# A two-layer encoder: first weights in three pieces, an earlier key remainder, and half of the up weights in other buffers

## The chip, the cores and the metric

The kernel runs on one core of one Trainium2 chip. The metric is the device time of one execution in microseconds (us); the time before is the median of three runs.

## The reference

Two layers, each a mixer (latent attention beside a convolution branch) and a gated feed-forward, on 1024 tokens of width 1024, all in float32; then a last RMS norm.

```python
p = rmsnorm(x, g_mix) @ w_in                       # queries' latent, keys' latent, key rope, conv input
c_q, c_kv = rmsnorm(p[..., :384]), rmsnorm(p[..., 384:640])
q, kv = c_q @ w_uq, c_kv @ w_ukv                   # 8 heads; k_nope and v come out of kv
y_attn = softmax(q k^T * scale) v
u = silu(layernorm(dwconv31(a * sigmoid(gt))))     # a, gt: the last columns of p
x = x + concat(y_attn, u) @ w_o
zg, zv = split(dwconv3(rmsnorm(x, g_ffn) @ w_up))  # 2 x 2816 columns
x = x + (silu(zg) * zv) @ w_down
```

## The kernel before

**Arithmetic.** A float32 product is made of three matrix products: weights and moving data are split into a high part (suffix h) and a remainder, or low part (suffix l), and hh, hl and lh are added up in PSUM. ACT casts the high part, DVE subtracts to get the low part (some weights go through ACT and an accumulating DMA of POOL instead). On TensorE (PE) nearly all matmuls are 128x128 by 128x512.

**Order of the work.** The order on PE, DVE, ACT and POOL is that in which the program is written (a planner keeps a clock for DVE in `project`, and a table of steps is filled by `put(step, rank, ...)` in the feed-forward). Only the order of SP, which issues the plain loads and stores, is set by a scheduler. An engine works strictly in its order, so an instruction that waits holds all that stand behind it.

**Buffers.** Large tiles lie in four pools of equal slots: "b" with 31 slots of 512 KB, "m" with 8, "wr" with 3, "ws" with 8 (`SLOTS`). A new tile takes the slot that its pool's plan gives it and waits until the last reader of the tile before it is through.

**Start** (`first_sections`, L398 to L510). Three weight blocks g0, a0 and g1 are loaded raw, cast and lowered in two column pieces, 0:256 (`some`) and 256:1024 (`rest`). x comes in eight blocks; `upper_x` (ACT, L432) and `lower_x` (DVE, L435) split block k into xs_kh and xs_kl. PE runs the products of block 0 for all three weights (L489), then block by block (L534).

**Keys** (`key` in `project`, L687 to L699). pk_j, the j-th of four products, is cast to kh_j by ACT (L692) and lowered to kl_j by DVE (L694). A step tells the planner of DVE how long it takes and after how long the next may follow; the `yield 0.0, 1.0` between cast and lowering lets it put one tap of the convolution (L1727, 1.28 us) between. pu, the next product, takes the PSUM buffer of pk_1. qss (L242) is the queries' sum of squares, which PE turns (rq0t, L261).

**Up stage** (`up_steps`, L1017 to L1224). The product with w_up is made for 22 column blocks f, each with seven half-size products i in the order 1, 5, 6, 3, 7, 2, 4 (12 matmuls each, so 84 per f), from sums and differences of quarters of the weights. `fetch(f, e)` (L1041) loads the two raw halves wu_f0 and wu_f1 into "wr" slots; `combine(f, ...)` (DVE, L1037) makes the differences in place, and the first of them, `combine(f, 0, 0, 2)`, needs both halves. `part` and `cast` make the split weights w_f_i. `evict` copies or adds a product's PSUM bank into zg_f and zv_f (ACT at L1096 to L1111, DVE at L1037); product 3 adds into the bank of product 5 and so cannot begin before `evict(5, f)` (ACT, L1099) has copied it. `filter_start`, `filter_tap`, `silu` and `close` make v_f, which SP stores (act<-v, L1136). Beside it DVE makes sums sd_j of the down weights, which SP loads (L1141) and stores again (ws<-sd, L1149).

A name such as wu0_140 in the orders below is layer 0, f = 14, half 0.

Of the kernel before, what the change touches and what calls it, by code (L numbers as in the profile page):

```python
# [16 lines left out]
T = 1024  # L17
# [65 lines left out]
HALVES = (slice(0, 512), slice(512, T))  # L83
# [38 lines left out]
class Encoder:  # L122
# [274 lines left out]
    def first_sections(self, l, supply):  # L397
        nc, par = self.nc, self.par[l]  # L398
        names = ("g0", "a0", "g1")
        w = [(self.tmp("wr", f"w{n}{l}r"), *(self.tmp("b" if n == "g0" else "ws", f"w{n}{l}{i}", F32R) for i in "hl"))  # L400
             for n in names]
        x, acc = [self.blk(f"x{k}") for k in range(8)], self.blk(f"xss{l}")
        hl = [[self.tmp("m", f"xs{l}_{k}{i}", F32R) if k >= 4 else self.blk(f"xs{l}_{k}{i}", F32R) for i in "hl"]
              for k in range(8)]
        ps = [self.wide(f"p{n}{l}") for n in names]
        every, left, right = slice(0, T), *HALVES
        some, rest = slice(0, 256), slice(256, T)
        nc.sync.dma_start(out=w[0][0][:, some], in_=self.weight_source(l, names[0])[:, some])
        warm = self.bank("warm")[:, 0:128]
        for _ in range(WARM):  # L410
            nc.tensor.matmul(warm, self.ones, self.ones, start=True, stop=True)
        nc.scalar.activation(out=self.cp.tile([128, 1], F32, name="table"), in_=self.ones[:, 0:1], func=AF.Square)

        def load(i, c):
            nc.sync.dma_start(out=w[i][0][:, c], in_=self.weight_source(l, names[i])[:, c])

        def load_x(k, c=every):
            nc.sync.dma_start(out=x[k][:, c], in_=self.xd[0][k][:, c])

        def cast(i, c, on_vector=False):  # L420
            raw, hi, _ = w[i]
            (nc.vector.tensor_copy if on_vector else nc.scalar.copy)(out=hi[:, c], in_=raw[:, c])

        def lower(i, c):
            raw, hi, lo = w[i]
            nc.vector.tensor_tensor(out=lo[:, c], in0=raw[:, c], in1=hi[:, c].bitcast(F32), op=ALU.subtract)

        def part(k, c):
            return self.first[:, 8:520] if k == 0 and c == left else x[k][:, c]

        def upper_x(k, c=every):
            nc.scalar.activation(out=hl[k][0][:, c], in_=part(k, c), func=AF.Copy, scale=self.first[:, k:k + 1])  # L432

        def lower_x(k, c=every):
            nc.vector.scalar_tensor_tensor(out=hl[k][1][:, c], in0=part(k, c), scalar=self.first[:, k:k + 1],  # L435
                                           in1=hl[k][0][:, c].bitcast(F32), op0=ALU.mult, op1=ALU.subtract)

        def square(k):
            for c in (left, right) if k == 0 else (every,):
                self.sumsq(acc[:, c], part(k, c), k, f"xsq{l}_{k}")  # L440

        load_x(0, right)
        load(1, some)
        load(2, some)
        load_x(1)
        load(2, rest)
        load(0, rest)
        load(1, rest)
        for k in range(2, 8):
            load_x(k)  # L450
        self.ident = self.const("ident", [128, 128], self.a["ident"])
        nc.vector.tensor_copy(out=self.ones_r, in_=self.ones)
        nc.sync.dma_start(out=self.par[0], in_=self.a["par"][0])
        self.par += [self.const(f"par{i}", [128, NPAR], self.a["par"][i]) for i in range(1, DEPTH)]
        self.gfin = self.const("gfin", [128, 8], self.a["g_final"])
        upper_x(0, left)
        cast(0, some, True)
        upper_x(0, right)
        cast(1, some)
        lower_x(0, left)  # L460
        lower_x(0, right)
        lower(0, some)
        lower(1, some)
        cast(2, some)
        lower(2, some)
        upper_x(1)
        lower_x(1)
        cast(2, rest)
        lower(2, rest)
        cast(0, rest)  # L470
        lower(0, rest)
        cast(1, rest)
        upper_x(2)
        lower(1, rest)
        lower_x(2)
        square(0)
        upper_x(3)
        lower_x(3)
        square(1)
        for k in range(4, 8):  # L480
            upper_x(k)
            lower_x(k)
            square(k - 2)
        square(6)
        square(7)
        w = [e[1:] for e in w]
        for i, p, q in ((0, 0, 0), (0, 0, 1), (1, 0, 0), (1, 0, 1), (0, 1, 0), (1, 1, 0), (2, 0, 0), (2, 0, 1), (2, 1, 0)):
            for c in HALVES:
                nc.tensor.matmul(ps[i][:, c], w[i][p][:, 0:128], hl[0][q][:, c], start=p + q == 0, stop=False)  # L489
        nc.gpsimd.tensor_copy(out=self.cp.tile([128, 1], F32, name="held"), in_=x[2][:, 0:1])  # L490
        order = [(1, i) for i in range(3)] + [(k, i) for k in range(2, 8) for i in range(3)]
        supply(-8.0, 8.0)
        for k, i in order:
            self.partial(ps[i], self.tiled(w[i]), hl, k, upper=i == 0 and k < 4)
            if (k, i) == (5, 2):
                dg = self.rsqrt_cols(acc, D, f"rx{l}", HALVES, self.bank, turned=True)
            if (k, i) == (6, 2):
                rx = self.blk(f"rx{l}")
                for s, r in zip(HALVES, self.spread(dg, f"rx{l}", HALVES, self.bank)):
                    nc.scalar.copy(out=rx[:, s], in_=r)  # L500
        supply(-8.0)
        return hl, rx, dict(zip(names, ps))
# [34 lines left out]
    def project(self, l, carry):  # L537
        nc, a = self.nc, self.a
# [3 lines left out]
        gates, ckv, kvs, cq, cqs, vs, w = {}, [], [], [], [], [], {}  # L542
# [144 lines left out]
        def key(j):  # L687
            if j == 0:
                heads.update((h, self.head_tiles(l, h)) for h in range(DIRECT))
            p = ps[f"k{j}"]  # L690
            kh, kl = self.blk(f"kh{l}_{j}", F32R), self.blk(f"kl{l}_{j}", F32R)
            nc.scalar.copy(out=kh, in_=p)  # L692
            yield 0.0, 1.0
            nc.vector.tensor_tensor(out=kl, in0=p, in1=kh.bitcast(F32), op=ALU.subtract)  # L694
            for i, s in enumerate((kh, kl)):
                self.move(kd[i][2 * j:2 * j + 2].rearrange("h d t -> (h d) t"), s)
                for h in range(DIRECT if j == 0 else 0):
                    self.move(heads[h][1][i][0:NOPE, :], s[h * NOPE:(h + 1) * NOPE, :])
                    self.move(heads[h][1][i][NOPE:96, :], krd[i])  # L699
            yield 1.22, 0.0  # L700
# [119 lines left out]
        hl, rx, ps = self.first_sections(l, supply) if l == 0 else self.next_sections(l, carry, supply)  # L820
# [208 lines left out]
    def up_steps(self, l, steps, put):  # L1029
        nc, a = self.nc, self.a  # L1030
        left, right = HALVES
# [7 lines left out]
        def fetch(f, e, tag="wr"):  # L1039
            raw[f][e] = self.tmp(tag, f"wu{l}_{f}{e}")  # L1040
            nc.sync.dma_start(out=raw[f][e], in_=a["w_up"][l, f + e * NF])  # L1041
# [4 lines left out]
        def combine(f, o, p, q, op=ALU.subtract):  # L1046
            z = quarters(f)
            sub(z[o], z[p], z[q], op)
# [12 lines left out]
        def cast(i, f):  # L1061
            e, h = {1: (0, 0), 2: (0, 1), 4: (1, 1)}[i]
            casts[i, f] = self.cast_pair(a["w_up"][l, f + e * NF][:, HALVES[h]], f"w{l}_{f}_{i}", "b" if i == 4 and f >= LEFT else "ws")
# [90 lines left out]
        for f in range(1, LEFT):  # L1154
            n = 10 + f if f == 1 else 11 + f
# [4 lines left out]
        for q, (i, f) in enumerate(seq):  # L1160
            n = base + q
# [13 lines left out]
        for f in range(LEFT, NF):  # L1175
            n = at[1, f]
            for e in range(2):
                put(n - 8, 5, lambda f=f, e=e: fetch(f, 1 - e))
            put(n - 5, 3, lambda f=f: combine(f, 0, 0, 2))
            put(n - 4, 3, lambda f=f: combine(f, 2, 2, 3, ALU.add))  # L1180
            put(n - 3, 2, lambda f=f: part(5, f))
            put(n - 3, 2.1, lambda f=f: combine(f, 2, 3, 0))
            put(n - 2, 2, lambda f=f: part(6, f))
            put(n - 2, 2.1, lambda f=f: combine(f, 1, 1, 2))
            put(n - 2, 2.2, lambda f=f: part(3, f))
            put(n - 1, 2, lambda f=f: part(7, f))
        for f in range(NF):
            n = max(at[2, f], at[3, f], at[6, f]) + 1
# [11 lines left out]
        for j in range(NF // 2):  # L1200
            n = at[1, 7 + j * 13 // 11]
# [688 lines left out]
```

## Time and profile before

| | us |
|---|---|
| median of 3 runs (range) | 2277.66 (2277.26 to 2278.66) |
| the profiled execution | 2278.46 |
| its span | 2276.7 |
| PE busy in the span | 2268.5 (100%) |
| DVE / ACT / POOL busy | 1722.5 / 1287.4 / 782.5 |

Of the profiled time, 1.76 us lie around the span. In a row of the timeline the first number is the start in us, the second the duration, then engine, line of the kernel and operation, out<-in, size and count; what stands in brackets is the idle time of that engine just before, and what ended it. PEld is the load of weights into PE, which runs ahead of the matmuls; an idle time on it that ends in another engine's work is a stall of PE. SPq is SP's issue of a DMA. A line's number can be that of a helper: L1037 is every DVE addition or subtraction of the up stage.

### The profile page before, as it was taken

Reading aid. Unit: us, or ns where it says so; the run is one execution under the profiler, and the core shown is the slowest. Engines: PE = TensorE matmul, PEld = TensorE weight load, DVE = VectorE, ACT = ScalarE, POOL = GpSimd, SP = SyncE. Lnnn points to the kernel's source line nnn. Section 1 sums busy time; section 2 is a strip of 40 time slices with the busy share of each in tenths; the row PEclk is TensorE's granted clock in tenths of the full one; section 3 lists DMA queues with packets and bytes.
Section 4 is the critical chain, followed back from the end, with each engine's and each line's share of the span. In section 5 each row is a group of like instructions: output and inputs, shape, how many; then the busy total and the mean of one; then the engine's idle time right before and its main releaser. Section 6 shows DMA issues by size and latency. Waiting matters only on the chain.

```text
span 2276.7 us, 30491 instructions
## 1 busy us (share of the span) xinstructions
PE 2268.5 (100%) x10682; PEld 1887.5 (83%) x10682; DVE 1722.5 (76%) x2296; ACT 1287.4 (57%) x2047; POOL 782.5 (34%) x812
## 2 busy tenths in 40 slices
PE   9999999999999999999999999999999999999998
PEld 8888888888888888888888888888888888888887
DVE  6988888768877776776559788886697777768765
ACT  5355877646655555544533468774475555555444
POOL 1222797532333333001412237873323333320032
PEclk9999999999999999999999999999999999999999
DMA  6889998856899998935968999967659999988356
GB/s 192 167 180 266 201 205 171 213 154 138 208 283 293 277 294 207 335 105 140 210 137 167 218 254 199 186 149 211 173 131 233 269 299 273 299 214 316 102 122 170
DMA packets 198713, 475.73 MB, mean 209 GB/s; under 512 B 27184, under 2 KB 34848, under 8 KB 198560
## 3 DMA queue, kind: packets, MB, share of 16 engines
q0 software_dynamic: 103136, 222.46, 48.7%
q1 hardware_dynamic: 95136, 250.80, 33.1%
q8 instruction: 84, 1.38, 0.2%
q14 instruction: 69, 0.57, 0.1%
q10 hardware_dynamic: 288, 0.53, 0.1%
HBM read 309.29 MB, written 80.40 MB: 171 GB/s over the span
## 4 chain that ended last, share of the span: by engine, by line
PE 91%; DVE 4%; DMA 2%; issue 2%; ACT 1%; POOL 0%; DVEq 0%; POOLq 0%; ACTq 0%; SPq 0%
PE p L1088 33%; PE pd L1276 18%; PE s L1529 8%; PE po L899 6%; PE o L1581 5%; PE t L1558 5%; PE pa L222 2%; PE pg L222 2%; DVE conv L1727 2%; PE pg L534 2%; PE pq L222 1%; PE pn L222 1%; PE pv L1507 1%; PE pkv L222 1%; PE pa L534 1%
## 5 line engine op out<-in xcount | busy, mean ns | idle before, releaser
L1088 PE MATMUL p<-b,w 128*128 128x512 f32 x3552 | 806.8, 389 | 0.3 <-DVE zv L1037 0.2
L1088 PEld LDWEIGHTS p<-b,w 128*128 128x128 f32 x3552 | 666.3, 188 | 140.2 <-DVE w L1467 0.8
L1276 PE MATMUL pd<-ab,wd 128*128 128x512 f32 (+1 forms) x1920 | 422.3, 381 | 0.0
L1276 PEld LDWEIGHTS pd<-ab,wd 128*128 128x128 f32 x1920 | 350.7, 188 | 69.5 <-DVE ab L1467 0.4
L186 POOL DMA_DIRECT2D w<-wu x96 | 84.9, 887 | 360.9 <-ACT w L185 319.2
L1529 PE MATMUL s<-k,q 96*128 96x512 f32 x768 | 207.6, 405 | 0.0
L1561 DVE TENSOR_TENSOR pt<-t,pt 128x512 fp32r<-128x512 f32 x256 | 165.0, 686 | 53.2 <-ACT pt L1560 51.8
L1744 POOL TENSOR_TENSOR late<-gate,par 128x1014 f32<-128x1014 f32 (+12 forms) x79 | 171.3, 2168 | 19.0 <-DVE qn L734 9.8
L1560 ACT CAST pt<-t 128x512 fp32r<-128x512 f32 x256 | 137.8, 589 | 66.2 <-PE t L1558 62.6
L1479 DVE SCALAR_TENSOR_TENSOR o<-zg,par,o 128x1023 f32<-128x1023 f32 x88 | 112.7, 1283 | 79.3 <-ACT o L1473 77.9
L186 POOL DMA_DIRECT2D w<-in_w_up x116 | 100.5, 866 | 198.7 <-ACT w L185 181.6
L1531 DVE TENSOR_REDUCE mx<-s 128x1 f32<-128x1024 f32 x128 | 155.7, 1216 | 0.6 <-PE s L1529 0.6
L1529 PEld LDWEIGHTS s<-k,q 96*128 96x128 f32 x768 | 135.4, 189 | 23.1
L1539 ACT ACTIVATE p<-s,mx 128x1024 f32<-128x1024 f32 x128 | 144.9, 1132 | 1.2 <-DVE mx L1531 1.2
L1727 DVE SCALAR_TENSOR_TENSOR conv<-gate,par,conv 128x1009 f32<-128x1009 f32 (+7 forms) x112 | 142.3, 1274 | 3.6 <-ACT conv L596 1.0
L1581 PE MATMUL o<-pt,v 128*128 128x512 f32 x512 | 140.8, 398 | 0.0
L862 POOL DMA_DIRECT2D wd<-in_w_down x44 | 33.0, 755 | 307.5 <-PE pd L1276 301.7
L1465 ACT CAST ab<-ac 128x512 fp32r<-128x512 f32 x130 | 80.0, 617 | 98.2 <-DVE ac L1211 95.5
L185 ACT ACTIVATE w<-w 128x512 fp32r<-128x512 f32 x212 | 133.6, 630 | 3.0
L1558 PEld LDWEIGHTS t<-ident,p 128*128 128x128 f32 x1024 | 119.9, 141 | 18.2 <-ACT p L1539 0.4
L1558 PE MATMUL t<-ident,p 128*128 128x128 f32 x1024 | 133.0, 273 | 0.0
L1037 DVE TENSOR_TENSOR zg<-p,zg 128x512 f32<-128x512 f32 x88 | 60.5, 689 | 89.4 <-PE p L1088 82.4
(2105 smaller groups left out, 4105.1 us busy)
## 6 DMA issues: line engine op xcount, KB each, us to landing
w<-in_w_up POOLq DMA_DIRECT2D x232, 256.0 KB, 7.3
wu<-in_w_up SPq DMA_DIRECT2D x88, 512.0 KB, 6.0
w<-wu POOLq DMA_DIRECT2D x96, 256.0 KB, 5.5
sd<-in_w_down SPq DMA_DIRECT2D x44, 512.0 KB, 10.3
ws<-sd SPq DMA_DIRECT2D x44, 512.0 KB, 7.9
wd<-in_w_down POOLq DMA_DIRECT2D x88, 256.0 KB, 5.4
act<-v SPq DMA_DIRECT2D x36, 512.0 KB, 5.8
ac<-act SPq DMA_DIRECT2D x72, 256.0 KB, 6.1
```

The source lines that it names most:

```text
L186: self.nc.gpsimd.dma_start(out=lo, in_=src, accum_op=ALU.add)
L222: nc.tensor.matmul(ps[:, HALVES[c]], w, x[:, HALVES[c]], start=(k == 0 and s == 0), stop=(k == n - 1 and s == 2))
L1088: nc.tensor.matmul(ps, w[p][:, k * 128:(k + 1) * 128], b[:, q], start=(i in (1, 5, 2) and k == 0 and t == 0), stop=(k == 3 and t == 2), sk ...
L1276: nc.tensor.matmul(ps[t, m][:, cs], w[i, j][p][:, m * 128:(m + 1) * 128], b[:, q, cs], start=(i in (1, 5, 2) and j == 0 and s == 0), stop= ...
L1529: nc.tensor.matmul(ps[:, cs], q[i][0:96, qs], k[j][0:96, cs], start=(s == 0), stop=(s == 2))
L1531: nc.vector.tensor_reduce(out=mx, in_=ps, op=ALU.max, axis=AX.X, negate=True)
L1539: nc.scalar.activation(out=p, in_=ps, func=AF.Exp, bias=mx, accum_out=st["sums"][:, qt:qt + 1])
L1558: nc.tensor.transpose(tp[:, i, qi * 128:(qi + 1) * 128], st["p"][2 * qp + qi][:, kt * 128:(kt + 1) * 128], self.ident)
L1561: nc.vector.tensor_tensor(out=lo, in0=tp, in1=hi.bitcast(F32), op=ALU.subtract)
L1581: nc.tensor.matmul(po, v[2 * c + i][:, h // 2, e, :], pt[s][:, i, :], start=(c == 0 and i == 0 and s == 0), stop=(c == 3 and i == 1 and s ...
L1727: self.nc.vector.scalar_tensor_tensor(out=y[:, lo:hi], in0=u[:, lo + s:hi + s], scalar=self.tap(l, j, t), in1=y[:, lo:hi], op0=ALU.mult, o ...
L1744: self.nc.gpsimd.tensor_tensor(out=p[:, lo:hi], in0=u[:, lo + s:hi + s], in1=self.tap(l, j, t).broadcast_to([128, hi - lo]), op=ALU.mult)
```

## The change

Four edits:

1. The raw weights of the start come in three column pieces (0:256, 256:512, 512:1024), so nine loads, casts and lowerings instead of six, and in another order between the loads of x.
2. The first products of blocks g0 and a0 run the left half of the columns first; the same 18 matmuls.
3. In `key`, the planner may lower kl_j at once (0.0) instead of 1.0 us after the cast.
4. For f from 4 on, `fetch` puts half 0 of the up weights into a "b" slot; half 1 stays in "wr".

```diff
-        some, rest = slice(0, 256), slice(256, T)
+        some, more, rest = slice(0, 256), slice(256, 512), slice(512, T)
...
+        load(1, some)
         load_x(0, right)
-        load(1, some)
         load(2, some)
         load_x(1)
-        load(2, rest)
-        load(0, rest)
-        load(1, rest)
-        for k in range(2, 8):
+        load(0, more)
+        load_x(2)
+        load(1, more)
+        load(2, more)
+        load_x(3)
+        for i in range(3):
+            load(i, rest)
+        for k in range(4, 8):
             load_x(k)
...
         upper_x(0, left)
         cast(0, some, True)
+        cast(1, some)
         upper_x(0, right)
-        cast(1, some)
         lower_x(0, left)
+        lower(0, some)
         lower_x(0, right)
-        lower(0, some)
         lower(1, some)
         cast(2, some)
         lower(2, some)
         upper_x(1)
         lower_x(1)
-        cast(2, rest)
-        lower(2, rest)
-        cast(0, rest)
-        lower(0, rest)
-        cast(1, rest)
+        cast(0, more)
+        lower(0, more)
         upper_x(2)
-        lower(1, rest)
         lower_x(2)
+        for i in (1, 2):
+            cast(i, more)
+            lower(i, more)
         square(0)
         upper_x(3)
         lower_x(3)
+        for i in range(3):
+            cast(i, rest)
+            lower(i, rest)
...
-        for i, p, q in ((0, 0, 0), (0, 0, 1), (1, 0, 0), (1, 0, 1), (0, 1, 0), (1, 1, 0), (2, 0, 0), (2, 0, 1), (2, 1, 0)):
-            for c in HALVES:
-                nc.tensor.matmul(ps[i][:, c], w[i][p][:, 0:128], hl[0][q][:, c], start=p + q == 0, stop=False)
+        begin = [(0, 0, 0, left), (1, 0, 0, left), (0, 0, 1, left), (1, 0, 1, left), (0, 0, 0, right), (1, 0, 0, right),
+                 (0, 1, 0, left), (0, 0, 1, right), (1, 0, 1, right), (0, 1, 0, right), (1, 1, 0, left), (1, 1, 0, right)]
+        for i, p, q, c in begin + [(2, p, q, c) for p, q in ((0, 0), (0, 1), (1, 0)) for c in HALVES]:
+            nc.tensor.matmul(ps[i][:, c], w[i][p][:, 0:128], hl[0][q][:, c], start=p + q == 0, stop=False)
...
             nc.scalar.copy(out=kh, in_=p)
-            yield 0.0, 1.0
+            yield 0.0, 0.0
             nc.vector.tensor_tensor(out=kl, in0=p, in1=kh.bitcast(F32), op=ALU.subtract)
...
-                put(n - 8, 5, lambda f=f, e=e: fetch(f, 1 - e))
+                put(n - 8, 5, lambda f=f, e=e: fetch(f, 1 - e, "b" if e else "wr"))
```

Three places of the order. First DVE around the keys of layer 0 (conv_3 are taps; line numbers after the change are 7 higher), before:

```order
L1727 SCALAR_TENSOR_TENSOR conv_3_845<-gate_3_777,par_63,conv_3_845 128x1018
L1727 SCALAR_TENSOR_TENSOR conv_3_845<-gate_3_777,par_63,conv_3_845 128x1019
L242 TENSOR_TENSOR qss_1127<-qss_1127,qss_2_1269 128x1024
L694 TENSOR_TENSOR kl_0_1290<-pk_1254,kh_0_1289 128x1024
L682 SCALAR_TENSOR_TENSOR cqs_2l<-cq_1267,par_63,cqs_2h 128x1024
L1727 SCALAR_TENSOR_TENSOR conv_3_845<-gate_3_777,par_63,conv_3_845 128x1020
L694 TENSOR_TENSOR kl_1_1321<-pk_1271,kh_1_1320 128x1024
L272 TENSOR_REDUCE rq0v<-rq0t 128x4 x2
```

and now:

```order
L1734 SCALAR_TENSOR_TENSOR conv_3_854<-gate_3_786,par_63,conv_3_854 128x1018
L701 TENSOR_TENSOR kl_0_1299<-pk_1263,kh_0_1298 128x1024
L242 TENSOR_TENSOR qss_1136<-qss_1136,qss_2_1278 128x1024
L689 SCALAR_TENSOR_TENSOR cqs_2l<-cq_1276,par_63,cqs_2h 128x1024
L701 TENSOR_TENSOR kl_1_1329<-pk_1280,kh_1_1328 128x1024
L701 TENSOR_TENSOR kl_2_1358<-pk_1315,kh_2_1357 128x1024
L272 TENSOR_REDUCE rq0v<-rq0t 128x4 x2
```

kl_0 now stands ahead of qss, and the taps of 1019 and 1020 columns come after kl_1 and the reduction. In layer 1 DVE's order is the same as before.

Second SP's order in the up stage of layer 0, before (act stores v_11, ws stores a sum):

```order
L1136 DMA act0_71<-v0_11_6710 128x1024
L1041 DMA wu0_140_6822<-in_w_up 128x1024
L1149 DMA ws0_73<-sd0_51_6603 128x1024
L1041 DMA wu0_151_6965<-in_w_up 128x1024
L1141 DMA sd0_60_6897<-in_w_down 128x1024
L1141 DMA sd0_61_6898<-in_w_down 128x1024
```

and now:

```order
L1143 DMA act0_71<-v0_11_6719 128x1024
L1048 DMA wu0_161_7125<-in_w_up 128x1024
L1156 DMA ws0_73<-sd0_51_6612 128x1024
L1048 DMA wu0_140_6831<-in_w_up 128x1024
L1148 DMA sd0_60_6906<-in_w_down 128x1024
L1148 DMA sd0_61_6907<-in_w_down 128x1024
```

Half 1 is now loaded for f = 16 where it was for f = 15, and stands ahead of half 0 for f = 14; the store of a sum stands ahead of that half too. Most blocks f from 8 on, in both layers, show the same exchange.

Third ACT in the up stage of layer 0, with what each row waits for in brackets (DMASW: a DMA that POOL issued), before:

```order
L1055 CAST w0_4_7_5441<-wu0_40_5296 128x512 [waits PE_49]
L185 ACTIVATE w0_4_7_5441<-w0_4_7_5441 128x512 [waits Activation_49]
L1473 ACTIVATE o0_2_5449<-zg0_2_5310,par0_63 128x1024 [waits DVE_49]
L1096 COPY zg0_4_5481<-p0_4_1_5451 128x512 [waits DVE_49,PE_49]
L1111 COPY zv0_2_5200<-p0_2_1_4942 128x512 [waits PE_49]
```

and now:

```order
L1062 CAST w0_4_7_5450<-wu0_40_5305 128x512 [waits PE_49]
L185 ACTIVATE w0_4_7_5450<-w0_4_7_5450 128x512 [waits Activation_49]
L1480 ACTIVATE o0_2_5458<-zg0_2_5319,par0_63 128x1024 [waits DVE_49]
L1103 COPY zg0_4_5490<-p0_4_1_5460 128x512 [waits DMASW5_49,DMASW3_49,PE_49]
L1118 COPY zv0_2_5209<-p0_2_1_4951 128x512 [waits PE_49]
```

The order is the same; zg_4 now takes the "b" slot that wu_40 had, and so waits for the two DMAs of POOL that read wu_40 last (w<-wu, L186). In layer 1 zg1_4 has the same wait.

## Rows read from the trace of the kernel before

**Rows 1.** The page, busy time of each engine: us, share of the span, instructions.

```profile
PE 2268.5 (100%) x10682; PEld 1887.5 (83%) x10682; DVE 1722.5 (76%) x2296; ACT 1287.4 (57%) x2047; POOL 782.5 (34%) x812
```

**Rows 2.** Timeline of PE's weight loads at the start.

```profile
10.77 0.30 PEld L534 LDWEIGHTS pg<-xs_1l,wg00h 128*128 128x128 f32 x2 [0.26 <-DVE xs_1l L435]
...
15.12 0.30 PEld L534 LDWEIGHTS pg<-xs_2l,wg00h 128*128 128x128 f32 x2 [0.38 <-DVE xs_2l L435]
```

**Rows 3.** Timeline of SP at the start.

```profile
0.74 0.38 SPq L408 DMA_DIRECT2D wg00r<-in_w_in  x1
1.18 0.42 SPq L418 DMA_DIRECT2D x<-in_x  x1
```

**Rows 4.** Timelines of ACT, DVE and PE's weight loads around the keys, layer 0.

```profile
163.77 0.99 ACT L692 CAST kh<-pk 128x1024 fp32r<-128x1024 f32 x1
...
165.19 1.22 DVE L242 TENSOR_TENSOR qss<-qss,qss 128x1024 f32<-128x1024 f32 x1
...
169.85 1.21 DVE L694 TENSOR_TENSOR kl<-pk,kh 128x1024 fp32r<-128x1024 f32 x1
...
166.47 1.03 PEld L261 LDWEIGHTS rq0t<-ident,qss 128*128 128x128 f32 x8
...
171.11 0.30 PEld L222 LDWEIGHTS pu<-cqs_0h,wu20h 128*128 128x128 f32 x2 [0.89 <-DVE kl L694]
```

**Rows 5.** Timeline of ACT early in the up stage, layer 0.

```profile
580.88 0.59 ACT L1096 COPY zg<-p 128x512 f32<-128x512 f32 x1 [1.03 <-DVE v L1037]
582.86 0.59 ACT L1111 COPY zv<-p 128x512 f32<-128x512 f32 x1 [1.40 <-PE p L1088]
...
585.85 1.06 ACT L1128 ACTIVATE o<-o 128x1024 f32<-128x1024 f32 x1 [0.74 <-DVE o L1479]
...
588.95 0.57 ACT L1099 COPY zv<-p 128x512 f32<-128x512 f32 x1
...
591.02 0.59 ACT L1103 COPY zg<-p 128x512 f32<-128x512 f32 x1 [0.97 <-PE p L1088]
```

**Rows 6.** Waits of SP's queue, 570 to 600 us: total, times, longest.

```profile
SPq L1041 <- DMA w<-wu: 4.9, 1, 4.9
```

**Rows 7.** Timeline of SP: the issue which that wait holds.

```profile
586.19 0.33 SPq L1041 DMA_DIRECT2D wu<-in_w_up  x1
```

**Rows 8.** Waits of SP's queue, 1700 to 1722 us (layer 1).

```profile
SPq L1041 <- DMA w<-wu: 3.4, 1, 3.4
```

**Rows 9.** Timeline of SP in the up stage, f = 18.

```profile
827.91 0.33 SPq L1041 DMA_DIRECT2D wu<-in_w_up  x1
829.59 0.33 SPq L1149 DMA_DIRECT2D ws<-sd  x1
```

**Rows 10.** Tile wu, 827.5 to 828.5 us: time of its one DMA from issue to landing.

```profile
DMA to landing us min/median/max: 9.5/9.5/9.5
```

**Rows 11.** Tile ws, 829 to 830 us: the same for its one DMA.

```profile
DMA to landing us min/median/max: 10.5/10.5/10.5
```

**Rows 12.** Timeline of DVE in the up stages (zg at 1855.51 and 1969.75: layer 1).

```profile
727.15 0.69 DVE L1037 TENSOR_TENSOR zg<-p,zg 128x512 f32<-128x512 f32 x1 [1.91 <-PE p L1088]
...
743.75 0.69 DVE L1037 TENSOR_TENSOR wu<-wu,wu 128x512 f32<-128x512 f32 x1 [3.02 <-DMA wu<-in_w_up]
...
747.96 0.68 DVE L1037 TENSOR_TENSOR zg<-p,zg 128x512 f32<-128x512 f32 x1
...
751.02 0.68 DVE L1037 TENSOR_TENSOR zv<-p,zv 128x512 f32<-128x512 f32 x1
...
841.94 0.69 DVE L1037 TENSOR_TENSOR zg<-p,zg 128x512 f32<-128x512 f32 x1
...
861.88 0.68 DVE L1037 TENSOR_TENSOR zg<-p,zg 128x512 f32<-128x512 f32 x1
...
1855.51 0.69 DVE L1037 TENSOR_TENSOR zg<-p,zg 128x512 f32<-128x512 f32 x1 [0.26 <-PE p L1088]
...
1969.75 0.69 DVE L1037 TENSOR_TENSOR zg<-p,zg 128x512 f32<-128x512 f32 x1 [1.09 <-PE p L1088]
```

**Rows 13.** Timeline of PE's weight loads in the up stage, f = 13.

```profile
751.75 0.30 PEld L1088 LDWEIGHTS p<-b,w 128*128 128x128 f32 x2 [0.66 <-DVE zv L1037]
```

## The prediction

> **What bounds the kernel now.** I read the busy times first: PE is busy 2268.5 us, 100% of the span, while DVE has 76%, ACT 57% and POOL 34% [rows 1]. The matmuls are the same before and after, so a gain can come only out of the idle time of PE, which is 2276.7 - 2268.5 = 8.2 us with its first wait and its last store in it; a loss can come from any of three engines and from the loads. So I went on to the places where PE's weight loads wait for another engine, at the four edits: two short waits at the start [rows 2], one at the keys [rows 4], one in the up stage of layer 0 [rows 13]. They sum to 0.26 + 0.38 + 0.89 + 0.66 = 2.2 us; this is all that the change could win. Then I read, in the up stages, how long each thing that PE uses was ready ahead: the waits of ACT, of SP's queue and of DVE [rows 5 to 8, 12].
>
> The sum is made against the profiled execution, 2278.46 us, which is 0.8 us above the median of 2277.66; the differences are added to the median. 0.2%, or 4.6 us, is about what a measurement of this kernel can tell from no change.
>
> **The change part by part.**
>
> *Start.* Three loads, three casts and three lowerings more; the bytes are the same. An issue costs SP 1.18 - 0.74 = 0.44 us [rows 3], so three cost at most 1.3 us if they stood on the path; they come between loads that are already in flight, and what stands ahead of x_1 is the same number of bytes. The wait of 0.26 us for xs_1l [rows 2] therefore stays. x_2 comes ahead of two weight pieces now, so the wait of 0.38 us for xs_2l [rows 2] should go; of what follows, PE must still wait for the same chain of lowerings on DVE later on, which has three instructions more. Bounds: -0.3 (the second wait goes) and +1.3 (three issues in line). I take **-0.1**, near the first, since nothing here waits for SP's issue itself.
>
> *Left half first.* The same 18 matmuls in another order; it lets PE begin g0 and a0 on the half that is loaded first. No time of its own beside the two waits above: nothing.
>
> *Key.* pu waits 0.89 us for kl_1, since it takes the buffer of pk_1 [rows 4]. With kl_0 and kl_1 ahead of taps that wait goes. But kl_0 must wait for kh_0, whose cast ends at 163.77 + 0.99 = 164.76 [rows 4], and qss now stands behind kl_0. So kl_0 runs from 164.8 to 166.0 and qss starts about 165.95 instead of 165.19, that is 0.76 later [rows 4]. PE turns qss right after it (rq0t, 166.47, with no wait in its row [rows 4]), so PE now waits 0.76 there, and reaches pu at about 171.0 instead of 171.11. The stall is moved, not removed: **-0.1**. Bounds: -0.85 if rq0t does not wait, +0.1 if it also meets kl_2, which stands ahead of the reduction now.
>
> *Up weights, the slot.* zg_4 of layer 0 is copied by ACT at 580.88 [rows 5]; now it takes the slot that wu_40 had. The same release can be seen before: SP's load that took the slot waited 4.9 us for the DMA w<-wu and was issued at 586.19 [rows 6, 7]. So ACT is held from 580.9 to 586.1, 5.2 us, and what is queued behind it is pushed. Its two idle times before the next thing that PE needs, 1.40 and 0.74 us [rows 5], take up 2.1, and 3.1 are left. The copy of product 5 into zv, at 588.95 to 589.52 [rows 5], would end at 592.6. PE adds product 3 into the same bank as soon as product 6 is done, which is what ends ACT's wait at 591.02 [rows 5]. So PE would stand 592.6 - 591.0 = **+1.6**. In layer 1 the same DMA is waited for 3.4 us instead of 4.9 [rows 8], 1.5 less; most of the stall is then covered, and I take **+0.4**. Bounds for both together: 0 (POOL's two DMAs land sooner) and +5 (nothing covers them).
>
> *Up weights, the loads.* This is the largest term. Before, SP issued wu_f0 first after the store act, when DVE released the "wr" slot. Now wu of f + 2, half 1, takes that slot and that place, then comes the store ws of a sum, then wu_f0. Against the whole period of seven loads and stores, wu_f0 has one transfer more ahead of itself, the ws. What this costs when the queue is full can be read for f = 18: wu_f0, issued at 827.91, landed 9.5 us later, at 837.4; ws, issued 1.68 us after it, landed 10.5 us later, at 840.1 [rows 9 to 11]. So in that stretch wu_f0 would come 2.7 us later. The Trainium skill, page DMA: Bandwidth & Descriptors, section Queues, rings and completion order, says that each DMA engine consumes descriptors in the order of the ring; these two landings agree, 2.7 us apart for one transfer.
>
> How much of it does PE feel? DVE's first combine of a block waits for wu_f0, and behind it on DVE stand zg and zv, which read PE's banks. For f = 13 DVE waited 3.02 us for the load, zg started at 747.96 and zv ended at 751.02 + 0.68 = 751.70 [rows 12], 3.74 us after; PE stood 0.66 us for it and so wanted zv at 751.09 [rows 13]. Where DVE is in time, zg itself waits for PE, as at 727.15 and (with no idle time worth a bracket, but in step) at 841.94 [rows 12]: six blocks in 114.79 us with the one stall of 0.66 in them, so 19.02 a block. For f = 13 PE had then finished zg's product at 727.15 + 19.02 = 746.17, 4.92 us before it wanted zv. DVE needs 3.74 of that, so **1.18 us** of lateness at zg are free, and the idle time of zg is free on top.
>
> With 2.7 us later each time: f = 13 pays all of it, 2.7 (it has no room left). f = 18 has 1.2 of room, so 1.5. f = 19 started zg at 861.88, against 841.94 + 19.02 = 860.96, so 0.26 of room and 2.45; but by then the stall before has given the queue 1.5 us, so 0.95. In layer 1 the first late block has 0.26 + 1.18 = 1.44 of room (zg at 1855.51 [rows 12]), so 1.25; the one after it is covered by that; the next has 1.09 + 1.18 = 2.27 (1969.75 [rows 12]), so 0.4. The other blocks have more room than 2.7. Sum: **+6.8**. Bounds: -0.66 (the loads come no later, and the stall of f = 13 goes too) and +12 (1 us later still in each, and no block helped by the stall before).
>
> *Sum:* -0.1 - 0.1 + 1.6 + 0.4 + 6.8 = +8.6 us. 2278.46 + 8.6 = 2287.1 for a profiled execution, 2277.66 + 8.6 = **2286.3 us** for the median.
>
> **The rivals.**
>
> *A: no load is late in a way that counts, and the small gains come in.* The point that decides is whether wu_f0 lands more than 1.2 us later at f = 13, 18 and 19. If a full queue is emptied earlier because half 1 no longer stands in the burst of ws and sd loads, wu_f0 comes no later, the 0.66 of f = 13 goes, the key's 0.85 and the start's 0.3 as well, and POOL's DMAs land ahead of zg_4. 2277.66 - 1.8 = 2275.9, not slower than before. For it: half 1 is now two blocks ahead, and only four to seven blocks in two layers have no room. Against: what leaves the burst comes back right ahead of wu_f0, so the bytes ahead of it are no fewer.
>
> *B: half of the lateness.* wu_f0 is issued behind ws but lands with it. Then 1.35 us later: f = 13 pays 1.35, f = 18 0.15, f = 19 1.1, the others nothing, 2.6 in sum, and 2277.66 - 0.2 + 2.0 + 2.6 = 2282.1. The same section of the Trainium skill says that completion is not in order of issue; by that rule this is what would come. The two landings above, in order of issue and a whole transfer apart, speak against it.
>
> *C: two transfers later.* If the queue is full from several blocks before, both the ws and the half-1 load ahead count, 5.4 us: f = 13 pays 5.4, f = 18 4.2, f = 19 the 0.95 left after that, layer 1 4.0 and 3.1 less what the block before gave, 14 to 16 in sum, so about 2293.
>
> *D: the change does little of what it says.* The key's wait only moves to rq0t; this is in my forecast already, worth 0.1 instead of 0.85.
>
> **How the numbers follow.** Forecast 0.46, with its own range of 2283 (two of the late blocks have more room) to 2291 (no help between blocks, +2.5, and a longer wait for the slot); A 0.31; B 0.16; C 0.06; faster by more than 4.6 us has 0.01, since all idle time at these places is 2.2 us. The range 2275 to 2291 takes in A, B and the forecast and leaves C out. Slower: 0.46 + 0.06 + half of B (its 2282.1 lies on the bound of 2282.2) 0.08 = 0.60; within 0.2%: 0.31 + 0.08 = 0.39; faster 0.01.
>
> **What the profile after would show.** Right: DVE's first combine waits for the load of wu in more than the three blocks of layer 0, with waits of 4 us and more at f = 13, 18 and 19; PE's weight loads wait for zv or zg behind them by 1 to 3 us each; ACT's copy of zg at 581 has an idle time of some 5 us that a DMA w<-wu ends; rq0t waits for qss, and pu for nothing. Wrong: wu landings of the full stretches no later than 9 to 11 us after the place where they were issued before, and no wait of DVE for them; then A holds. If PE's idle time grows without a late wu, the slot of zg_4 or another "b" slot was mis-sized.

## The result and the profile after

| | before | after |
|---|---|---|
| median of 12 runs (range), us | 2277.70 (2276.95 to 2278.66) | 2283.47 (2280.69 to 2285.00) |
| ratio, 95% interval | | 1.0024 (1.0015 to 1.0033) |
| the profiled execution, its span | 2278.46, 2276.7 | 2280.69, 2278.9 |

The change makes the kernel 5.8 us slower, and its runs lie 4.3 us apart where those of before lie 1.7 apart. The profiled execution is the fastest of the twelve: it shows where the time is lost, but less of it than the median has.

PE's busy time on the page is that of before [rows 1], so the loss is idle time of PE:

```profile
PE 2268.7 (100%) x10682; PEld 1888.0 (83%) x10682; DVE 1725.5 (76%) x2299; ACT 1288.6 (57%) x2050; POOL 783.5 (34%) x812
```

The timeline of PE's weight loads after the change has four idle times worth naming, which answer to [rows 4, 13]:

```profile
166.50 0.86 PEld L261 LDWEIGHTS rq0t<-ident,qss 128*128 128x128 f32 x8 [0.35 <-DVE qss L242]
...
591.79 1.23 PEld L1095 LDWEIGHTS p<-b,w 128*128 128x128 f32 x6 [2.21 <-ACT zv L1106]
...
1704.60 1.48 PEld L1095 LDWEIGHTS p<-b,w 128*128 128x128 f32 x7 [1.16 <-DVE zg L1044]
...
1721.82 2.37 PEld L1095 LDWEIGHTS p<-b,w 128*128 128x128 f32 x11 [0.99 <-ACT zv L1106]
```

The waits of 0.26 and 0.38 us at the start [rows 2], of 0.89 at pu [rows 4] and of 0.66 at f = 13 [rows 13] are gone. In their place stand 2.21 us at 591, as forecast, and 1.16 and 0.99 us in layer 1; all of them lie where the blocks f = 3 and f = 4 meet, in each layer. Nothing of the kind stands at f = 13, 18 or 19, where I had expected most of the loss. The wait of 0.66 at f = 13 is no sure sign of the change, though: of the six kernels below that keep the old order of the loads from f = 8 on (`e_nowu`, `e_only4`, `e_slot3`, `e_slot4`, `e_key`, `e_start`), none shows it in its trace.

ACT's timeline shows what holds PE. The rows at 585.45 and 591.15 answer to [rows 5]; the one at 564.48 is an earlier copy, of zg_3, which waits for a DMA of POOL too. What that second wait costs I saw only after the first set of experiments.

```profile
564.48 0.59 ACT L1103 COPY zg<-p 128x512 f32<-128x512 f32 x1 [2.34 <-DMA w<-wu]
...
585.45 0.59 ACT L1103 COPY zg<-p 128x512 f32<-128x512 f32 x1 [3.71 <-DMA w<-wu]
...
591.15 0.59 ACT L1106 COPY zv<-p 128x512 f32<-128x512 f32 x1
```

And DVE does wait for the up weights much more often than before. The waits of DVE from 560 to 930 us (line, releaser, total, times, longest), first before:

```profile
DVE wu L1037 <- DMA wu<-in_w_up: 7.3, 3, 3.0
```

and after:

```profile
DVE wu L1044 <- DMA wu<-in_w_up: 21.2, 11, 4.2
```

So the loads are late, eleven times in layer 0, and PE does not feel it in this execution. I had said 4 us and more at f = 13, 18 and 19; DVE waits 0.97, 1.52 and 2.29 us there, and the 4.2 is at f = 14. For the median of +5.8 the first set weighs theory **T**, that the slot under zg_4 and the late loads both cost (my forecast), against rival **R**, that the slot alone does. The second set weighs what was left by then: theory **S**, that two "b" slots which POOL's DMAs still read, that of wu_20 under zg_3 and that of wu_40 under zg_4, make the whole loss, against rival **L**, that the order of the later loads makes it.

### The profile page after: what moved, and what is told of

Same layout as the page of the kernel before. It is cut to its first block, busy times and chain, and to the rows that moved or that the text cites. A ratio compares the mean times of both kernels' runs of the same rounds, so it can differ in the third digit from the quotient of the medians.

```text
span 2278.9 us, 30488 instructions
## 1 busy us (share of the span) xinstructions
PE 2268.7 (100%) x10682; PEld 1888.0 (83%) x10682; DVE 1725.5 (76%) x2299; ACT 1288.6 (57%) x2050; POOL 783.5 (34%) x812
## 4 chain that ended last, share of the span: by engine, by line
PE 93%; issue 2%; DMA 1%; ACT 1%; DVE 1%; POOL 0%; POOLq 0%; DVEq 0%; ACTq 0%
PE p L1095 31%; PE pd L1283 18%; PE s L1536 8%; PE po L906 7%; PE o L1588 5%; PE t L1565 5%; PE pq L222 3%; PE pa L222 3%; PE pkv L222 2%; PE pg L222 2%; PE pg L541 2%; PE pn L222 1%; DMA w<-wu 1%; PE pv L1514 1%; PE pk L222 1%
## 5 line engine op out<-in xcount | busy, mean ns | idle before, releaser
L186 POOL DMA_DIRECT2D w<-wu x96 | 85.0, 889 | 316.6 <-ACT w L185 258.8
L186 POOL DMA_DIRECT2D w<-in_w_up x116 | 100.6, 867 | 207.2 <-ACT w L185 188.9
L1044 DVE TENSOR_TENSOR wu<-wu,wu 128x512 f32<-128x512 f32 x132 | 90.5, 688 | 46.3 <-DMA wu<-in_w_up 43.7
```

The source lines that it names most:

```text
L186: self.nc.gpsimd.dma_start(out=lo, in_=src, accum_op=ALU.add)
```

## Experiments

Each kernel was timed in five rounds beside the kernel before, on the same chip (6 to 11 executions of each). The medians of before were 2277.99, 2278.30 and 2277.73 us in the three sets of four.

**Set 1: the change without its fourth edit, the fourth edit alone, and two ways to free zg_4's slot.**

`e_nowu` is the change with `fetch(f, 1 - e)` as before.

> The change without its fourth edit (all up weights stay in wr). PE reaches the up stage of layer 0 0.97 us earlier in the trace of the change than before (534.42 against 535.39), and nothing else of the first three edits lies behind that. Both theories: 2277.7 - 1.0 = 2276.7, ratio to before 0.9994 to 0.9998, runs as close together as those of before (2 us). If the start or the key had a hidden cost later on: over 2278.

2277.55 us, 0.9997 (0.9988 to 1.0005). The first three edits do no harm; the gain that both theories gave them (2276.7) is not shown either, since the interval takes in no change.

`e_wu` is the kernel before with the fourth edit:

```diff
-                put(n - 8, 5, lambda f=f, e=e: fetch(f, 1 - e))
+                put(n - 8, 5, lambda f=f, e=e: fetch(f, 1 - e, "b" if e else "wr"))
```

> The fourth edit alone on the kernel before. Both theories: the whole loss is its own, so 2277.7 + 5.8 + 1.0 = 2284.5, with runs some 4 us apart as with the whole change. If the start edits share in the loss (three more loads): under 2282.

2283.78 us, 1.0025 (1.0015 to 1.0035): the whole loss is in this line. Its profiled execution, 2286.15 us, is the longest of its eight, and shows all four stalls large (PE's weight loads):

```profile
575.27 1.91 PEld L1088 LDWEIGHTS p<-b,w 128*128 128x128 f32 x9 [1.00 <-DVE zg L1037]
...
593.90 3.27 PEld L1088 LDWEIGHTS p<-b,w 128*128 128x128 f32 x15 [2.43 <-ACT zv L1099]
...
1707.07 1.91 PEld L1088 LDWEIGHTS p<-b,w 128*128 128x128 f32 x9 [1.79 <-DVE zg L1037]
...
1725.49 2.81 PEld L1088 LDWEIGHTS p<-b,w 128*128 128x128 f32 x8 [2.23 <-ACT zv L1099]
```

They sum to 7.5 us, against a span 2284.4 - 2276.7 = 7.7 us longer than before. That the two are so near is in part chance: behind the fourth stall PE ran at half its clock, which lost some 1.5 us more (last section), and the 0.66 of [rows 13] is not there.

`e_skip4` is the whole change with one block excepted:

```diff
-                put(n - 8, 5, lambda f=f, e=e: fetch(f, 1 - e, "b" if e else "wr"))
+                put(n - 8, 5, lambda f=f, e=e: fetch(f, 1 - e, "b" if e and f > LEFT else "wr"))
```

> The whole change, but half 0 of block f = 4 stays in wr, so that zg_4 takes no slot that a DMA of POOL still reads. Theory T (the slot and late loads both cost): the stalls of 2.2 us at 591 and about 1 us at 1721 go, the loads remain, 2283.5 - 3.2 = 2280.3 and the runs still 3 to 4 us apart. Rival R (the slot alone costs, and its DMA lands at different times from run to run): 2276.5, runs within 2 us.

2277.51 us, 0.9999 (0.9990 to 1.0008), runs within 2.4 us. One block of 22 carries the loss; the 17 others, with the new order of the loads, cost nothing. Rival R's 2276.5 is 1.0 us off and T's 2280.3 is 2.8 us off, so T fell: what it held the late loads for is not there. By the order of ACT this edit frees the slots under zg_3 and zg_4 both, so it does not tell the two apart.

`e_early` fetches half 0 two steps earlier in all blocks: `put(n - (10 if e else 8), ...)` with the fourth edit's slots.

> The whole change with half 0 fetched two steps earlier (n - 10), so that SP issues wu_f0 ahead of act and not behind ws; zg_4 has no such slot here either. Theory T: the late loads go too, no wait of DVE for wu over 1 us, 2276 to 2276.7, runs within 2 us, 3.5 to 4 us below the variant that only frees zg_4. Rival R: the same as that variant, within 0.7 us.

2283.40 us, 1.0026 (1.0015 to 1.0036): a miss for T and R. zg_4 has a free slot here, but zg_3 has not (ACT's copy waits 2.14 us for a DMA w<-wu), and the earlier tile takes another slot that is busy: now SP's load of wu_50 waits 5.2 us for a DMA w<-wu of POOL, DVE waits 5.99 us for that load, and PE stands 3.93 us behind DVE. DVE's row, then PE's:

```profile
592.63 0.69 DVE L1044 TENSOR_TENSOR wu<-wu,wu 128x512 f32<-128x512 f32 x1 [5.99 <-DMA wu<-in_w_up]
...
602.42 1.68 PEld L1095 LDWEIGHTS p<-b,w 128*128 128x128 f32 x8 [3.93 <-DVE zv L1044]
```

In layer 1 two more stalls of PE follow, 0.97 us behind zg and 1.27 behind zv. It is the same kind of loss in another place: what decides is which old tile the plan of the pool puts under the new one.

**Set 2: the two slots apart, and the order of the loads alone.** All four are one line on the kernel before. `e_only4` has half 0 of f = 4 alone in "b" (`"b" if e and f == LEFT else "wr"`).

> The kernel before, with half 0 of block f = 4 alone in b (all later blocks as before, so the order of the loads from f = 8 on is unchanged). Theory S (two b slots that POOL's DMAs still read, that of wu_20 under zg_3 and that of wu_40 under zg_4, make the whole loss): stalls of PE at about 575, 592, 1706 and 1724 as in the trace of the fourth edit alone (1.0 + 2.4 + 1.8 + 2.2 = 7.3 us; 4.4 in the trace of the whole change), so 2282.4 to 2285.3. Rival L (the order of the later loads makes it): within 1 us of before, 2277 to 2279.

2284.06 us, 1.0027 (1.0015 to 1.0038). SP's order from f = 8 on is that of before here, and the loss is the whole loss. Rival L falls. Three of the four stalls that S named are in the trace (2.66 us at 593, 1.04 at 1708, 2.00 at 1726); at 575 PE waits only 0.20 us, though ACT's copy of zg_3 waits there too (2.39). So a copy that comes late makes a stall in some executions and not in others.

`e_slot3` puts half 1 of f = 4 into "b" and half 0 into "wr" (`"wr" if e or f > LEFT else "b"`).

> The kernel before, with half 1 of f = 4 in b and half 0 in wr: by the order ACT's copy of zg_3 has the slot of wu_20 and waits for its DMA, zg_4 has a free one. Theory S: the stalls of PE for zg (at 575 and 1706) remain, those for zv (592, 1724) go, +1.2 to +2.8 us: 2279 to 2281. If the first wait pushes ACT far enough to make the second stall as well: 2282 or more. Rival L: 2277 to 2279.

2279.70 us, 1.0006 (0.9997 to 1.0015), so +1.4 us, in the range that S gave. Its rows: ACT's copy of zg_3, DVE's zg behind it, and PE's stall in each layer.

```profile
565.95 0.59 ACT L1096 COPY zg<-p 128x512 f32<-128x512 f32 x1 [2.89 <-DMA w<-wu]
...
566.57 0.69 DVE L1037 TENSOR_TENSOR zg<-p,zg 128x512 f32<-128x512 f32 x1 [2.40 <-ACT zg L1096]
...
574.87 1.22 PEld L1088 LDWEIGHTS p<-b,w 128*128 128x128 f32 x6 [0.71 <-DVE zg L1037]
...
1704.09 1.93 PEld L1088 LDWEIGHTS p<-b,w 128*128 128x128 f32 x9 [1.25 <-DVE zg L1037]
```

The interval takes in no change at all, so the size is open between -0.7 and +3.4 us; that the slot makes these two stalls is in the rows.

`e_slot4` fetches half 0 of f = 4 into "b" two steps later (`put(n - (6 if e and f == LEFT else 8), ...)`).

> The kernel before, with half 0 of f = 4 in b, fetched two steps later: zg_3 has a free slot, zg_4 has that of wu_40 and waits for its two DMAs. Theory S: the stalls for zv (592 and 1724) remain, those for zg go, +3 to +4.6 us: 2281 to 2282.6, and this and the other half together give the loss of the variant with both. My own sum on record had only this slot, at +2.0: 2280. Rival L: 2277 to 2279.

2282.75 us, 1.0022 (1.0013 to 1.0030), so +4.5 us. With the +1.4 of the other slot this makes +5.9, against +5.8 with both; each of the two terms is known to some 2 us only. Again ACT's copy, then PE's stalls in the two layers:

```profile
587.52 0.59 ACT L1096 COPY zg<-p 128x512 f32<-128x512 f32 x1 [4.05 <-DMA w<-wu]
...
593.86 5.32 PEld L1088 LDWEIGHTS p<-b,w 128*128 128x128 f32 x17 [2.76 <-ACT zv L1099]
...
1725.72 1.46 PEld L1088 LDWEIGHTS p<-b,w 128*128 128x128 f32 x7 [2.02 <-ACT zv L1099]
```

These are 4.8 us, but the span is 2283.0 - 2276.7 = 6.3 longer. The rest is in the clock after the first stall (last section). How much of the median's +4.5 is the clock is open, since one execution alone has a trace.

`e_from5` has half 0 in "b" from f = 5 on (`"b" if e and f > LEFT else "wr"`): the new order of the loads and nothing else.

> The kernel before with half 0 in b from f = 5 on and nothing else: the new order of the loads alone, no slot that POOL reads under zg_3 and zg_4. Theory S: no stall of PE for wu although DVE waits for it in ten or more blocks of a layer, 2277 to 2278.5. My sum on record (the loads cost 6.8): 2284.8. Rival L: 2282 to 2284.

2278.17 us, 1.0001 (0.9992 to 1.0010). DVE waits for wu twelve times in layer 0, 20.1 us in all, and no stall of PE comes of it there; in layer 1, with twelve waits of 24.8 us in all, one does, 0.71 us at 1728 behind zv. The waits of layer 0:

```profile
DVE wu L1037 <- DMA wu<-in_w_up: 20.1, 12, 2.5
```

The stretch that I had reckoned with, f = 18, in this kernel: SP's issue of act, half 1, ws and half 0, then the landing of that act (its tile, from issue), then DVE's combine and zg.

```profile
825.88 0.33 SPq L1136 DMA_DIRECT2D act<-v  x1
827.72 0.33 SPq L1041 DMA_DIRECT2D wu<-in_w_up  x1
829.40 0.33 SPq L1149 DMA_DIRECT2D ws<-sd  x1
829.89 0.33 SPq L1041 DMA_DIRECT2D wu<-in_w_up  x1
```

```profile
DMA to landing us min/median/max: 5.2/5.2/5.2
```

```profile
836.83 0.69 DVE L1037 TENSOR_TENSOR wu<-wu,wu 128x512 f32<-128x512 f32 x1 [1.54 <-DMA wu<-in_w_up]
...
841.74 0.69 DVE L1037 TENSOR_TENSOR zg<-p,zg 128x512 f32<-128x512 f32 x1 [0.62 <-issue]
```

wu_f0 is issued at 829.89, 2.0 us later than before, and yet is there at 836.8, where before it landed at 837.4 [rows 9, 10]. The same act took 8.8 us to land before and takes 5.2 here. Half 1 (512 KB) no longer goes out in the burst with ws and two sd: before, that load (issued at 819.34, landed at 827.3), ws and the two sd were all issued in the 7 us ahead of act, and the first sd landed at 831.3; here ws goes out at 816.28 and has landed at 822.2, and when act is issued the two sd alone of SP's transfers are in flight, the second of which lands at 828.8. What is issued behind them then lands sooner too: half 1 after 4.6 us and wu_f0 after 6.9, against 9.5 for wu_f0 before.

**Set 3: the first three edits apart, and two candidates.** `e_key` is the third edit alone.

> The third edit alone on the kernel before. In the trace of the whole change PE goes from its first product of a key (pk) to pu in 11.94 us against 12.83 before, 0.89 less. If that is the edit's own: the same 0.9 less here from pk to pu, and 2277.7 - 0.9 = 2276.8 to 2277.5, too little to tell from before in time. My step on record (the wait only moves to rq0t): at most 0.1 less from pk to pu.

2276.84 us, 0.9996 (0.9987 to 1.0005). Too little to tell by the time; the trace shows where the wait goes. First weight loads in the timelines, us:

| | pk | rq0t | pu | pk to pu |
|---|---|---|---|---|
| before | 158.28 | 166.47 | 171.11 | 12.83 |
| e_key | 158.13 | 166.64 | 170.11 | 11.98 |
| e_start | 157.88 | 166.04 | 170.53 | 12.65 |

Its rows: DVE's kl_0, then PE at rq0t and at pu.

```profile
164.23 1.23 DVE L694 TENSOR_TENSOR kl<-pk,kh 128x1024 fp32r<-128x1024 f32 x1 [0.84 <-ACT kh L692]
...
166.64 0.86 PEld L261 LDWEIGHTS rq0t<-ident,qss 128*128 128x128 f32 x8 [0.40 <-DVE qss L242]
...
170.11 0.41 PEld L222 LDWEIGHTS pu<-cqs_0h,wu20h 128*128 128x128 f32 x2
```

kl_0 waits for kh_0, as I had said; qss and rq0t come late, but by 0.40 us and not 0.76, and pu waits for nothing. Against the profiled execution of before the edit wins 0.85 us of PE's time, but that execution is the longest from pk to pu of all that have no third edit. Over the fourteen kernels with a trace, the seven with the edit take 11.8 to 12.5 us from pk to pu (mean 12.08; rq0t waits 0.14 to 0.79) and the seven without it 12.3 to 12.8 (mean 12.53; pu waits 0.58 to 0.93). So the gain is some 0.45 us in the mean, and the two groups overlap.

`e_start` is the first and second edits alone.

> The first and second edits alone. In the trace of the whole change PE reaches the first key product at 158.03 against 158.28, 0.25 earlier; step on record: 0.1 to 0.3. So pk 0.1 to 0.4 earlier and pu 0.1 to 0.4 earlier, time within 0.5 us of before. If three loads more cost their issues in line: 1.3 us later.

2277.46 us, 0.9998 (0.9989 to 1.0007). PE comes to pk 0.40 us earlier than before (table), the top of that range; in `e_from5`, whose start is that of before, it came to pk at 159.02, 0.74 later than before, and in `e_slot4` at 159.32. So 0.4 us is inside what the start varies by from one execution to the next, and one trace does not show the gain. The fourteen together do in part: the wait for xs_2l is in all seven that have the old start (0.23 to 0.56 us) and in none of the seven with the new one, and these come to pk 0.48 us earlier in the mean (158.08 against 158.56), with overlap. A cost of 1.3 us is not there.

`e_from8` is the whole change with `"b" if e and f > LEFT + 3 else "wr"`.

> Candidate: the whole change with half 0 in b only from f = 8 on, so no slot of the first blocks changes hands. Theory S: start and key keep their 1.0 us, no stall of PE for zg or zv near 575, 591, 1704, 1721, and none for wu: 2276.5 to 2277.3. If the loads cost after all: over 2279.

2277.28 us, 0.9997 (0.9988 to 1.0006). No stall is left near 575, 591, 1704 or 1721. PE now waits 0.92 us at 535.55 behind ACT's copy of zv, early in the up stage, where the kernel before has no such wait in its trace; so a part of what PE wins earlier is lost again there (1.04 in `e_skip4`, 0.48 in `e_start`; but none in the whole change or `e_nowu`, and 0.60 in `e_only4`, which has the old start).

`e_from8_early` is that with `put(n - (10 if e and f > LEFT + 3 else 8), ...)`.

> The same candidate with half 0 fetched two steps earlier (n - 10) from f = 8 on: DVE waits for wu less than 2 us in a layer, against 20 us with the change. Theory S: the waits had room, so the time is that of the candidate before within 0.7 us, 2276 to 2277.3. If late loads do cost a part of the time in most runs: 1 us or more below it.

2277.39 us, 0.9999 (0.9990 to 1.0007). DVE does not wait for a load of wu at all in either layer, against 18.8 us in layer 0 of the candidate before it, and the time is the same: what DVE waits for wu was free. Neither candidate can be told from the kernel before: the medians of the four kernels with the first three edits and without the loss lie 0.3 to 0.5 us below theirs, and each interval takes in no change.

## Why the prediction was right or wrong

The total was forecast as +8.6 and is +5.8; the direction and the range hold. That the sum came so near is luck: its largest term is not there, and the term that makes the loss was put at a third of its size. The runs show which steps failed.

- **Start**, -0.1: the step stands, a little small. The wait for xs_2l goes, and that for xs_1l stays in three of the seven traces with the new start (0.25 to 0.54), as I had said; the gain is 0.48 us in the mean at pk, after two of the seven have lost 0.41 and 0.85 us at the sums of x (rx0t).
- **Key**, -0.1: the mechanism is there (kl_0 waits 0.84 us for kh_0, and rq0t for qss), the size is not: some -0.45 in the mean of the traces. I put both waits from one execution. In `e_key` DVE and ACT came to that place 0.4 us earlier against PE, and rq0t waited 0.40 us and not 0.76; in `e_skip4` and `e_from8_early` it did wait 0.72 and 0.79.
- **The slot**, +2.0 in both layers: the mechanism was right, mis-sized and incomplete. zg_4's slot alone measured +4.5 (ratio 1.0013 to 1.0030). The DMA that ACT waits for landed later than the one that I read: ACT's copy came at 587.52 in `e_slot4`, 1.4 after the 586.1 that I took from [rows 6, 7], and PE itself was 0.6 us later there (its first up product at 504.84 against 504.27), so 0.8 of it counts. That kernel also fetches half 0 later; in `e_wu`, which does not, the copy comes at 587.56 all the same. (In the profile of the whole change the two stalls behind zg_4 are 2.21 and 0.99, 3.2 in sum.) A fall of the clock, worth some 1.5 us where it comes (last section), had no term in my sum. In layer 1, where I let 1.5 us of a shorter wait cover nearly all, the stall is 2.02. And I missed that the other slot, wu_20 under zg_3, changed hands too: +1.4. One line of a pool's plan moved two neighbours.
- **The loads**, +6.8, the largest term: wrong. I took the spacing of two landings in a full stretch as what one more transfer ahead of wu_f0 costs in every late block, and wrote against rival A that what leaves the burst comes back right ahead of wu_f0. It does, but when fewer transfers are in flight: act lands in 5.2 us and not 8.8, and wu_f0 of f = 18 comes 0.6 us earlier than before. At f = 13, which was to pay 2.7, I took the 0.66 of one execution to mean that no room was left. Where a load is late, DVE's free time covers it, but for the 0.71 us at 1728: `e_from5` is at 1.0001 and `e_from8_early`, without any such wait, no faster. The measured term is 0 (-1.8 to +2.3 us by the interval). Rival A was right in this part, and wrong in the whole, since the slots cost more than I gave them. The Trainium skill, page DMA: Bandwidth & Descriptors, section Queues, rings and completion order, says that on each DMA engine descriptors are consumed in the order of the ring. The landings of `e_from5` agree with it: act at 831.1, half 1 at 832.3 and wu_f0 at 836.8, in the order of their issue.

So the runs put 0 and +5.9 in the place of +6.8 and +2.0, and some -0.45 in the place of the key's -0.1. Right in my reasons were the place of the stall at 591, the chain that makes it (a DMA of POOL, ACT's copy of zg_4, ACT's copy of zv, product 3) and that nothing in the first three edits costs; and I had written that, should PE's idle time grow without a late wu, a "b" slot was mis-sized; that is what came. Rival B's 2282.1 lies nearer to the measured time than my forecast, but by chance as well: its 2.6 us for the loads are not there either. Most of the sum was put in the wrong place.

## What to carry to other kernels

When a tile moves to another pool, do not ask first what it gains there: list for every tile of that pool whose turn changes which old tile lies under it and who reads that last. A slot that was released by an engine and is now released by a DMA can make whatever engine writes it next wait for a landing (here ACT, 2.1 to 4.2 us), with all that stands behind it. A later place in the queue cost nothing by itself here; ask how many transfers are in flight at that moment, and take the landing time of the transfer just ahead as the measure. And read a wait of under 1 us in more than one execution before a sum is built on it: those at the start, at the keys and at f = 13 differed by 0.3 to 0.7 us from trace to trace.

## What the runs showed that I had not expected

After a stall of 2.76 us PE ran at half its clock for about 3 us. The view by windows of `e_slot4` (busy time and count of PE, PEld, DVE, ACT, POOL; then granted clock, DMA share, GB/s):

```profile
590.00:593.80 3.80, 1.52 (x7) 0.94 (x5) 2.61 (x3) 3.80 (x7) 1.04 (x2) 1.00 0.41 66
593.80:595.00 1.20, 1.14 (x5) 0.97 (x6) 1.20 (x2) 1.20 (x4) 1.06 (x2) 1.00 0.10 17
595.00:598.00 3.00, 3.00 (x9) 2.38 (x8) 2.12 (x3) 2.40 (x3) 2.15 (x4) 0.52 0.81 126
598.00:602.00 4.00, 4.00 (x18) 3.20 (x18) 3.56 (x5) 0.62 (x1) 0.00 (x0) 0.93 0.85 234
```

PE is fed without a gap from 595 to 598, but 9 matmuls fall into these 3.00 us and 18 into the 4.00 behind them; the granted clock is 0.52, the lower of its two levels (1.2 and 2.4 GHz) for nearly all of that stretch, and full again soon behind it. Half the work of 3 us is lost, an estimate of some 1.5 us, and with it the spans agree: 4.8 us of stalls and 1.5 make the 6.3 by which this execution is longer (PE's later start of 0.6 us and the 0.66 at f = 13, which is not there, cancel).

Two other traces show the same, `e_only4` after the stall of 2.66 us at 593 (clock 0.51 from 595 to 598) and `e_wu` after its fourth stall, of 2.23 us at 1725:

```profile
1727.00:1729.00 2.00, 2.00 (x6) 1.51 (x6) 1.75 (x2) 2.00 (x3) 1.77 (x4) 0.50 0.94 116
```

The 2.21 us at 591 in the profile of the whole change, the 2.43 us in that of `e_wu`, the 2.02 us in that of `e_slot4` and even the 3.93 us in that of `e_early` were not followed by it:

```profile
600.00:604.00 4.00, 1.58 (x7) 1.32 (x8) 4.00 (x6) 0.44 (x2) 0.00 (x0) 1.00 0.49 199
```

So the length of a stall alone does not decide. A stall of 2 to 4 us cost its own length in some executions and some 1.5 us more in others, and part of the spread of the runs (4.3 us after, 1.7 before) may be this; that it is was not tried.
